# Attention products for heads of 64 value columns: two side-by-side parts in one stationary tile, two products instead of three

## The chip, the cores and the metric

The kernel runs on one core of one Trainium2 chip. Five engines of that core matter here: TensorE (PE; its weight loads are shown apart as PEld), VectorE (DVE), ScalarE (ACT), GpSimd (POOL) and SyncE (SP), which issues the weight transfers. The metric is the device time of one execution in microseconds (us).

## The reference

Two transformer blocks follow one another on one sequence of 512 tokens of width 1024, all in float32. What matters here is cut down to the attention of 64-wide heads:

- Block 1, branch a: 8 heads of 64 (block-sparse attention over two blocks of 256 tokens, causal, with a linear distance bias); with 512 tokens every earlier block is selected, so each head is plain causal attention. Branch b: 4 heads whose values are 128 wide (the difference of two softmaxes).
- Block 2: 4 heads of chunked gated linear attention whose values are 128 wide, and 8 heads of 64 (causal attention with a bias that counts three dilated windows).

```
p = softmax(q k^T / 8 + bias)          # per head, 512 x 512, causal
y[t, d] = sum_s p[t, s] v[s, d]        # d = 0..63 for the 16 heads of 64
```

Before and after the attention stand dense products (projections, gates, output products, two feed-forward layers of 2816).

## The kernel before

All tensors lie feature-major (features on the partitions, 512 tokens in the columns). To keep float32 accuracy on TensorE's faster fp32r path, every operand is split into an exact high and low part: ACT casts the high part (`nc.scalar.copy`), DVE subtracts it for the low part (`sub`, line 125). A product of two split operands is three TensorE products, hi·hi, hi·lo and lo·hi (`mm3`, line 142), each issued by `mm` (line 134, its instruction has line 137).

The weights of all dense products come as one stream of 512 KB chunks on SP's queue, and each half chunk is split by ACT (line 251) and DVE (line 125) up to three halves ahead of its use.

TensorE's order is fixed by the program (`pin` chains every PE instruction to the one before). It is worked out by a planner: tasks (generators) yield the time after which their next piece should be ready, `pump` issues the first task that is ready by the planner's clock `self.pt`, and fills with dense tile products when none is. `self.pt` grows by an estimated cost per PE instruction: for a product of n moving columns max(0.106, 0.216 n/512) us, for a transpose 0.108. ACT, DVE and POOL run their own queues in order, in an order that the framework sets from its own estimates; it need not be that of the program text.

For one 64-wide head the steps are these:

- `v_parts` (line 394) takes a projected value tile of two heads from PSUM. After four transposes into a `pt` bank, ACT casts `vh` (line 410, 128x512) and DVE subtracts for `vl`; both are token-major, 128 columns per block of 128 tokens, 64 for each head of the pair.
- `scores` and `normalise` make the probabilities `p` (one of three SBUF tiles of 1280 columns, handed on by `drop`).
- `att_v` (line 457) has four turns j = 0..3, one for each block of 128 keys. `turn(j)` transposes the probabilities of those keys into a `pt` bank (4 - j transposes), ACT casts them to `ph` (line 468) and DVE subtracts for `pl`. The turns 0 and 1 are issued ahead; then `av(j)` (line 452) adds three products into the single `y` bank, with 64 columns of `vh` or `vl` as the stationary tile and 512, 384, 256 and 128 moving columns for j = 0..3; after it `turn(j + 2)` is issued.
- At the end of a head ACT casts the high part of `y[:64]` (lines 556 in block 1, 1318 in block 2) and DVE subtracts for the low part, into the half `own` of the pair's tiles; then `p` is dropped and the next head may start its `att_v` (the resource `pv` is 1).

The heads with 128 value columns (`diff` in block 1, `gla` in block 2) use the same `av` with 128 stationary columns. In block 2 the last output product takes the eight k tiles in the order in which they are made, so the two products of the last pair of heads (`out`, line 1377) wait for the last head.

```
        qs = slice(128 * j, 512)
        c = slice(128 * j + cols.start, 128 * j + cols.stop)
        self.mm3(y[:, qs], (v[0][:, c], v[1][:, c]), (ph[:, qs], pl[:, qs]), j == 0, j == TB - 1)
...
            yield from self.att_v(p, box["v"], slice(64 * e, 64 * e + 64), y[:64])
            nc.scalar.copy(yh[own], y[:64])
            self.sub(yl[own], y[:64], yh[own])
```

Of the kernel before, what the change touches and what calls it, by code (L numbers as in the profile page):

```python
# [13 lines left out]
ALU = mybir.AluOpType  # L14
# [5 lines left out]
TB = S // 128  # L20
# [22 lines left out]
# cost of a transpose on the tensor engine, for the order in which its work is issued  # L43
# [3 lines left out]
class Done:  # L47
    """Marks a piece of work as issued; `at` is when its result should be there."""
# [10 lines left out]
class Item:  # L59
    """A dense tile product: runs whenever no task has tensor work that is ready."""  # L60
# [5 lines left out]
class Emitter:  # L66
# [25 lines left out]
    def phase(self, order=range(NSLOT)):  # L92
        """A part of the program with its own use of the working tiles."""
        self.slot, self.turn, self.free = {}, {}, list(order)
        self.pfree, self.pslot, self.res["prob"] = [0, 1, 2], {}, 3

    def W(self, tag, dt=F32, b=1, shape=(128, 512)):
        """A working tile; `b` of a tag take turns."""
        n = self.turn[tag] = self.turn.get(tag, -1) + 1
        key = (tag, n % b)  # L100
        if key not in self.slot:
            self.slot[key] = self.free.pop(0)
        return self.t(self.work, list(shape), dt, f"w{self.slot[key]}")

    def prob(self):
        """A tile for the probabilities of a head; free again after drop."""
        i = self.pfree.pop(0)
        p = self.t(self.work, [128, PW], F32, f"p{i}")
        self.pslot[id(p)] = i, p
        return p  # L110
# [31 lines left out]
    def mm3(self, out, l, r, first=True, last=True):  # L142
        """out (+)= l^T r from exact parts, (hi, lo) each."""
        self.mm(out, l[0], r[0], first, False)
        self.mm(out, l[0], r[1], False, False)
        self.mm(out, l[1], r[0], False, last)

# [61 lines left out]
    def pump(self, stop=None):  # L209
        """Issue until `stop()` (default: no tasks and no dense work are left)."""  # L210
# [29 lines left out]
    def _split(self, h):  # L240
        """Exact parts of half a chunk."""
# [30 lines left out]
    def mtile(self, ps, w, m, rhs, evac):  # L272
        """Generator: ps = W[:, m]^T rhs, then evac(ps); yields after each k."""
        n = len(rhs)
        for k in range(n):
            if k == 0 and ps is None:
                ps = self.bank()
            self.kstep(ps, w, m, k, rhs[k], k == 0, k == n - 1)
            yield 0.0
        return evac(ps)  # L280

    def kouter(self, cols, rhs, tags=("mm", "mm", "s", "s")):
        """Several tiles at once, k outermost: starts as soon as rhs[0] is there."""
        ps = [self.bank(tags[i]) for i in range(len(cols))]
        n = len(rhs)
# [10 lines left out]
    def colsum(self, ps, sq, first=True, last=True, c=0, tbs=range(TB)):  # L296
        """ps[:, 8 c + 2 tb] += per-token sums over the partitions of sq = (hi, lo), whose columns
        begin with the first of the token tiles tbs; the odd columns get the same."""
# [6 lines left out]
    def parts(self, full, dst=None):  # L305
        """(hi, lo) of a tile, for its sums."""
# [5 lines left out]
    def squares(self, x):  # L312
        """(hi, lo) of x^2, for its sums."""
        return self.parts(self.square(x))

    def gather(self, acc, sq):
        """acc += sq, beside the products; the first piece is the accumulator itself."""
# [5 lines left out]
    def after(self, ins, first):  # L323
        """Issue `ins` behind `first` on the engine that both run on."""
        self.tc.add_manual_dep(ins.ins, first.ins.name, NOSYNC, reason="order")

    def sums(self, ps, n=1, tbs=range(TB)):
        """The per-token sums that colsum left in the first n groups of columns."""
# [10 lines left out]
    def bcast(self, r):  # L339
        """[128 tokens, n] -> [128, 128 n], the same value on all partitions."""  # L340
# [34 lines left out]
    def qk_pair(self, q32, k32):  # L375
        """Stacked exact parts of two heads (rows 0-63 and 64-127) for the score products."""
# [17 lines left out]
    def v_parts(self, ps, rb=None, dst=None):  # L394
        """Task: token-major exact parts of a feature-major value tile in PSUM."""
# [8 lines left out]
        def go():  # L404
# [5 lines left out]
            nc.scalar.copy(vh, pt)  # L410
            self.sub(vl, pt, vh)
# [3 lines left out]
    def scores(self, h, qk, bias, out):  # L415
        """Task part: unnormalised probabilities [128, 1280] and 1/sum of one head."""
# [35 lines left out]
    def av(self, y, j, v, cols, ph, pl):  # L452
        qs = slice(128 * j, 512)
        c = slice(128 * j + cols.start, 128 * j + cols.stop)
        self.mm3(y[:, qs], (v[0][:, c], v[1][:, c]), (ph[:, qs], pl[:, qs]), j == 0, j == TB - 1)

    def att_v(self, p, v, cols, y):
        """Task part: y[d, q] = sum_s v[s, d] p[q, s] for one head."""
# [18 lines left out]
        for j in range(TB):  # L477
            self.av(y, j, v, cols, *parts[j])
# [5 lines left out]
    def block1_mix(self):  # L484
# [37 lines left out]
        def e_v(box):  # L522
            def f(ps):
                box["v"], g = self.v_parts(ps, rbx["b"])
# [15 lines left out]
        def moba(j, e, box):  # L540
# [12 lines left out]
            yield from self.att_v(p, box["v"], slice(64 * e, 64 * e + 64), y[:64])  # L553
            own = slice(64 * e, 64 * e + 64)
            yh, yl = ya[j]
            nc.scalar.copy(yh[own], y[:64])
            self.sub(yl[own], y[:64], yh[own])
# [4 lines left out]
        def diff(j, box):  # L562
# [23 lines left out]
            yield from self.att_v(p1, box["v"], slice(0, 128), y)  # L586
# [20 lines left out]
        # start: the first pair with k outermost, while x arrives; the norm follows  # L607
# [6 lines left out]
        for k, _ in enumerate(self.mtile(self.bank("s"), "w_in", 24, h, e_gate(0))):  # L614
# [4 lines left out]
            if k == 5:  # L619
# [4 lines left out]
                e_v(box[0])(ps[2])  # L624
# [6 lines left out]
        # lambda, the same on every partition  # L631
# [33 lines left out]
        for j in range(1, 8):  # L665
# [5 lines left out]
            self.dense(self.mtile(None, "w_in", o + 8 + jj, h, e_v(box[j])), gate)  # L671
# [33 lines left out]
    def bridge(self, w, rhs, g, slots, evac, chain, cols, h, tags=("mm", "s", "s", "y"), made=()):  # L705
        """The eight tiles of rhs @ W, the last g of them for the first and then for the other half of
        the tokens, and with h the first four tiles of the next stage, likewise: what the norm of one
        half waits for lies beside products of the other half. The weights of tiles that are used
        twice stay in `slots`. evac(m, c, ps) takes a tile (its columns c); chain(t, ps, done) is the
        task that takes the last tile of a half and makes that half of h; `made` are banks with the  # L710
        first tiles."""
# [65 lines left out]
    def block1_rest(self, mg):  # L777
# [98 lines left out]
        # modulation of block 2 on the vector engine, beside the products  # L876
# [49 lines left out]
        def chain(t, c, ps, done):  # L926
# [18 lines left out]
            # x + f g r has the squares' sum |x|^2 + 2 r x.fg + r^2 |fg|^2  # L945
# [39 lines left out]
    def ada(self, k, x, rb, i, dst, t=None):  # L985
        """Exact parts of x * rb * gm + shift, per feature."""
# [8 lines left out]
    def headsum(self, ps, sq):  # L995
        """ps[:, 2 tb + e] = per-token sums over the two halves of the partitions."""
# [4 lines left out]
    def block2_mix(self, x, h, ps):  # L1001
# [28 lines left out]
        # queries and keys of the linear attention, then its gates: 16 columns, all k in one tile  # L1030
# [74 lines left out]
        def gla(p):  # L1105
# [15 lines left out]
            def decayed(s):  # L1121
                """Keys of the first halves and queries of the second halves of all 2s tokens,
                decayed to and from the end of the first half."""
# [22 lines left out]
            def near(s, b):  # L1146
                """Parts for the pairs within 128 tokens; the queries of the two heads in columns
                of their own, with zeros in the other head's rows."""
# [19 lines left out]
            # the diagonal  # L1168
# [34 lines left out]
            for e in range(2):  # L1203
# [26 lines left out]
                for j in range(TB):  # L1230
                    self.av(y, j, gv[hd], slice(0, 128), *parts[j])
# [58 lines left out]
        def e_av(box):  # L1290
            def f(ps):
                box["v"], g = self.v_parts(ps)
# [3 lines left out]
        def dilated(j, e, box):  # L1296
# [16 lines left out]
            yield from self.att_v(p, box["v"], slice(64 * e, 64 * e + 64), y[:64])  # L1313
            if ya[j] is None:
                ya[j] = T(f"yah{j}", F32R), T(f"yal{j}", F32R)
            own = slice(64 * e, 64 * e + 64)
            yh, yl = ya[j]
            nc.scalar.copy(yh[own], y[:64])  # L1318
            self.sub(yl[own], y[:64], yh[own])
# [54 lines left out]
        # the first two tiles of the last product, their k in the order in which it comes  # L1374
# [147 lines left out]
def stream(inp, order):  # L1522
    """The 128x128 tiles of all dense weights in the order in which they are used."""
    w2 = inp["w_in_2"][0]
    w2 = np.concatenate([w2[:, :1536], w2[:, 1552:]], axis=1)
    # columns of block 2: gq gk gv gr aq ak av
# [11 lines left out]
def layout(g):  # L1538
# [16 lines left out]
    # constants of the shapes: key position minus query position, masked above the diagonal  # L1555
    d = (np.arange(512)[None, :] - np.arange(128)[:, None] - 384)
    o["dmast"] = np.where(d <= 0, d, -1e30).astype(np.float32)
    # eight times the log of how many of the three dilated windows hold the distance
# [3 lines left out]
    # pairs (key, query) of a 128-token block whose last common block of 2s tokens splits between them  # L1562
# [33 lines left out]
```

## Time and profile before

| | |
|---|---|
| time, median of 3 runs | 1505.06 us (1501.72 to 1508.11) |
| span of the profiled execution | 1504.9 us |
| mean granted TensorE clock | 0.985 |
| PE busy | 1451.4 us (96%), 7054 products and transposes |
| DVE busy | 934.4 us (62%) |
| ACT busy | 708.5 us (47%) |
| POOL busy | 307.7 us (20%) |
| DMA | 154.38 MB, mean 103 GB/s |

The span runs from the first to the last instruction of one profiled execution, on which all rows below are taken; it lies 0.2 us below the median of the runs. "Busy" counts the time in which at least one instruction of the engine was under way. PE's products are pipelined and overlap, so what one product costs the stream is read from start to start and not from its duration.

### The profile page before, as it was taken

Reading aid. Unit: us, or ns where it says so; the run is one execution under the profiler, and the core shown is the slowest. Engines: PE = TensorE matmul, PEld = TensorE weight load, DVE = VectorE, ACT = ScalarE, POOL = GpSimd, SP = SyncE. Lnnn points to the kernel's source line nnn. Section 1 sums busy time; section 2 is a strip of 40 time slices with the busy share of each in tenths; the row PEclk is TensorE's granted clock in tenths of the full one; section 3 lists DMA queues with packets and bytes.
Section 4 is the critical chain, followed back from the end, with each engine's and each line's share of the span. In section 5 each row is a group of like instructions: output and inputs, shape, how many; then the busy total and the mean of one; then the engine's idle time right before and its main releaser. Section 6 shows DMA issues by size and latency. Waiting matters only on the chain.

```text
span 1504.9 us, 19407 instructions
## 1 busy us (share of the span) xinstructions
PE 1451.4 (96%) x7054; PEld 1180.6 (78%) x7054; DVE 934.4 (62%) x1753; ACT 708.5 (47%) x1370; POOL 307.7 (20%) x285
## 2 busy tenths in 40 slices
PE   7999999999999999999998879899999999999998
PEld 6777777788988777888797667777779888888887
DVE  6655665656468888542548697766656766665322
ACT  5656655553643222332336546576546444444221
POOL 5322122101261111110314343412210111111000
PEclk9999999999999999999999987999999999999999
DMA  4221222224307887333234101121222233333331
GB/s 168 71 71 56 70 71 70 84 84 154 127 29 231 270 271 248 112 99 97 85 107 146 42 29 41 30 85 50 77 86 69 86 97 98 98 99 98 119 112 64
DMA packets 44592, 154.38 MB, mean 103 GB/s; under 512 B 5088, under 2 KB 5616, under 8 KB 44496
## 3 DMA queue, kind: packets, MB, share of 16 engines
q1 hardware_dynamic: 42944, 148.41, 31.6%
q0 software_dynamic: 1408, 4.59, 1.0%
q8 instruction: 55, 0.90, 0.2%
q14 instruction: 41, 0.34, 0.1%
q10 hardware_dynamic: 144, 0.14, 0.0%
HBM read 148.93 MB, written 4.19 MB: 102 GB/s over the span
## 4 chain that ended last, share of the span: by engine, by line
PE 74%; DVE 10%; issue 5%; DMA 4%; ACT 3%; POOL 3%; SPq 0%; DVEq 0%; POOLq 0%; ACTq 0%
PE mm L137 59%; PE s L137 8%; PE y L137 3%; DMA p<-w_ada 3%; DVE w L125 2%; PE pt L140 2%; POOL w L320 1%; DMA wraw<-w 1%; DVE wlo L125 1%; PE pc L137 1%; DVE w L891 1%; PE pt L137 1%; DVE w L1113 1%; ACT whi L251 1%; POOL rr L336 0%
## 5 line engine op out<-in xcount | busy, mean ns | idle before, releaser
L137 PE MATMUL mm<-hh,whi 128*128 128x512 f32 x1096 | 449.4, 410 | 12.6 <-ACT hh L370 7.0
L125 DVE TENSOR_TENSOR wlo<-wraw,whi 128x512 fp32r<-128x512 f32 x410 | 297.5, 729 | 252.4 <-ACT whi L251 248.7
L251 ACT CAST whi<-wraw 128x512 fp32r<-128x512 f32 x410 | 250.5, 620 | 399.4 <-PE mm L137 284.7
L137 PE MATMUL mm<-hl,whi 128*128 128x512 f32 x1096 | 431.3, 394 | 0.0
L137 PE MATMUL mm<-hh,wlo 128*128 128x512 f32 x1096 | 431.3, 394 | 0.0
L137 PE MATMUL mm<-w,whi 128*128 128x512 f32 (+1 forms) x984 | 281.5, 371 | 2.2 <-ACT w L1318 0.9
L137 PEld LDWEIGHTS mm<-hh,whi 128*128 128x128 f32 x1096 | 207.7, 189 | 69.5 <-issue 20.5
L137 PEld LDWEIGHTS mm<-hh,wlo 128*128 128x128 f32 x1096 | 207.7, 190 | 45.1
L137 PEld LDWEIGHTS mm<-hl,whi 128*128 128x128 f32 x1096 | 208.2, 190 | 36.2 <-DVE hl L371 0.6
L137 PEld LDWEIGHTS mm<-w,whi 128*128 128x128 f32 x984 | 177.4, 188 | 34.7 <-ACT w L1318 1.3
L137 PE MATMUL mm<-w,wlo 128*128 128x512 f32 (+1 forms) x492 | 181.5, 369 | 1.6 <-DVE wlo L125 1.6
L137 PEld LDWEIGHTS mm<-w,wlo 128*128 128x128 f32 x492 | 92.7, 188 | 17.5 <-DVE wlo L125 2.0
L137 PE MATMUL s<-w,w 128*128 128x128 f32 (+3 forms) x364 | 94.4, 352 | 8.1 <-DVE w L1196 5.2
L125 POOL TENSOR_TENSOR w<-w,w 64x512 fp32r<-64x512 f32 x48 | 66.6, 1387 | 142.4 <-ACT w L384 92.5
L137 PEld LDWEIGHTS s<-w,w 128*128 128x128 f32 x364 | 62.1, 206 | 39.8 <-issue 31.9
L891 DVE SCALAR_TENSOR_TENSOR w<-p,p 128x1024 bf16<-128x1024 f32 x48 | 63.7, 1327 | 20.5 <-DMA p<-w_ada 20.2
L125 DVE TENSOR_TENSOR w<-pt,w 128x512 fp32r<-128x512 f32 (+3 forms) x106 | 52.9, 505 | 34.5 <-ACT w L468 29.0
L1453 POOL TENSOR_TENSOR w<-w,w 128x512 f32<-128x512 f32 x22 | 29.0, 1319 | 205.6 <-ACT w L1452 205.5
L428 DVE CUSTOM_DVE_ANT_0 p<-s,w 128x128 f32<-128x128 f32 (+1 forms) x96 | 46.8, 488 | 35.4 <-PE s L137 34.7
L848 POOL TENSOR_TENSOR w<-w,w 128x512 f32<-128x512 f32 x22 | 28.6, 1304 | 193.6 <-ACT w L847 193.6
L320 POOL TENSOR_TENSOR w<-w,w 128x256 f32<-128x256 f32 (+1 forms) x43 | 48.8, 1138 | 91.6 <-ACT w L355 56.7
L125 DVE TENSOR_TENSOR w<-w,w 128x512 fp32r<-128x512 f32 (+3 forms) x107 | 59.5, 567 | 11.3 <-ACT w L859 4.8
(273 smaller groups left out, 1910.2 us busy)
## 6 DMA issues: line engine op xcount, KB each, us to landing
wraw<-w SPq DMA_DIRECT2D x220, 512.0 KB, 3.6
p<-w_ada SPq DMA_DIRECT2D x48, 512.0 KB, 4.4
x<-xT SPq DMA_DIRECT2D x8, 256.0 KB, 6.2
x<-xT POOLq DMA_DIRECT2D x8, 256.0 KB, 2.9
xd<-x SPq DMA_DIRECT2D x8, 256.0 KB, 2.5
x<-xd POOLq DMA_DIRECT2D x8, 256.0 KB, 2.9
outT<-x SPq DMA_DIRECT2D x7, 256.0 KB, 2.1
p<-c SPq DMA_DIRECT2D x1, 512.0 KB, 3.6
```

What stands on the lines that cost most here:

```text
L125: (eng or self.nc.vector).tensor_tensor(out=out, in0=full, in1=hi, op=ALU.subtract)
L137: self.pin(self.nc.tensor.matmul(out, lhsT=lhsT, rhs=rhs, start=start, stop=stop), us)
L140: self.pin(self.nc.tensor.transpose(out, in_, self.ident), USTR)
L251: self.nc.scalar.copy(hi, raw)
L320: self.nc.gpsimd.tensor_tensor(out=acc, in0=acc, in1=sq, op=ALU.add)
L428: nc.vector.tensor_tensor_reduce(out=p[:, OFF[i]:OFF[i] + w], in0=ps[:, :w], in1=bias[:, 384 - 128 * i:512], op0=ALU.add, op1=ALU.max, sca ...
L848: nc.gpsimd.tensor_tensor(out=g, in0=g, in1=sg, op=ALU.mult)
L891: nc.vector.scalar_tensor_tensor(out=junk, in0=wa, scalar=1.0, in1=cond, op0=ALU.mult, op1=ALU.mult, accum_out=self.mod[:, ni:ni + 1])
L1113: nc.vector.tensor_tensor_scan(c[:, o:o + n], self.one256[:, :n], la[p][:, o:o + n], 0.0, op0=ALU.mult, op1=ALU.add)
L1453: nc.gpsimd.tensor_tensor(out=u, in0=u, in1=sg, op=ALU.mult)
```

## The change

For the 16 heads of 64 value columns, the high and the low part of a head's values are laid side by side: 64 columns of high part and 64 of low part make one stationary tile of 128 columns for each block of 128 keys. `v_parts(heads=True)` now fills `vh` with head 0 (high and low) and `vl` with head 1, in four smaller operations instead of two. `av` then issues two products for each j, the tile with `ph` and with `pl`, instead of three; rows 0 to 63 of the `y` bank hold (vh·ph + vh·pl) and rows 64 to 127 hold (vl·ph + vl·pl). The new `y_parts` adds the two halves at the end: ACT copies the lower half to SBUF (into the head's own `p` tile), DVE adds the upper half, and high and low part are then cast and subtracted from that sum. The 128-wide heads keep three products. Besides, docstrings and comments are blanked.

```diff
-    def v_parts(self, ps, rb=None, dst=None):
+    def v_parts(self, ps, rb=None, dst=None, heads=False):
...
-            nc.scalar.copy(vh, pt)
-            self.sub(vl, pt, vh)
+            if heads:
+                pv = pt.rearrange("p (t e d) -> p t e d", e=2, d=64)
+                for e, t in enumerate((vh, vl)):
+                    tv = t.rearrange("p (t s d) -> p t s d", s=2, d=64)
+                    nc.scalar.copy(tv[:, :, 0], pv[:, :, e])
+                    self.sub(tv[:, :, 1], pv[:, :, e], tv[:, :, 0])
+            else:
+                nc.scalar.copy(vh, pt)
+                self.sub(vl, pt, vh)
...
-    def av(self, y, j, v, cols, ph, pl):
+    def av(self, y, j, v, ph, pl):
         qs = slice(128 * j, 512)
-        c = slice(128 * j + cols.start, 128 * j + cols.stop)
-        self.mm3(y[:, qs], (v[0][:, c], v[1][:, c]), (ph[:, qs], pl[:, qs]), j == 0, j == TB - 1)
+        c = slice(128 * j, 128 * j + 128)
+        if len(v) == 2:
+            self.mm3(y[:, qs], (v[0][:, c], v[1][:, c]), (ph[:, qs], pl[:, qs]), j == 0, j == TB - 1)
+        else:
+            self.mm(y[:, qs], v[0][:, c], ph[:, qs], j == 0, False)
+            self.mm(y[:, qs], v[0][:, c], pl[:, qs], False, j == TB - 1)
+
+    def y_parts(self, y, p, own, dst):
+        nc = self.nc
+        lo, y32 = p[own, :512], p[own, 512:1024]
+        nc.scalar.copy(lo, y[64:])
+        nc.vector.tensor_tensor(out=y32, in0=y[:64], in1=lo, op=ALU.add)
+        nc.scalar.copy(dst[0][own], y32)
+        self.sub(dst[1][own], y32, dst[0][own])
...
-            yield from self.att_v(p, box["v"], slice(64 * e, 64 * e + 64), y[:64])
-            own = slice(64 * e, 64 * e + 64)
-            yh, yl = ya[j]
-            nc.scalar.copy(yh[own], y[:64])
-            self.sub(yl[own], y[:64], yh[own])
+            yield from self.att_v(p, box["v"][e:e + 1], y)
+            self.y_parts(y, p, slice(64 * e, 64 * e + 64), ya[j])
             self.drop(p)
```

The last group stands once in `moba` (block 1) and once, in the same way, in `dilated` (block 2).

## Rows read from the trace of the kernel before

**Rows 1.** PE's busy time on the profile's page: us, share of the span, instructions.

```profile
PE 1451.4 (96%) x7054; PEld 1180.6 (78%) x7054; DVE 934.4 (62%) x1753; ACT 708.5 (47%) x1370; POOL 307.7 (20%) x285
```

**Rows 2.** Windows: length; busy us of PE, PEld, DVE, ACT, POOL; clock; DMA share; GB/s.

```profile
60.00:180.00 120.00, 119.41 (x576) 90.53 (x576) 71.04 (x159) 76.74 (x157) 26.22 (x18) 1.00 0.22 66
900.00:1090.00 190.00, 183.06 (x911) 142.71 (x910) 129.31 (x306) 115.50 (x261) 56.67 (x53) 0.92 0.19 56
1090.00:1103.00 13.00, 10.08 (x50) 6.28 (x51) 6.41 (x14) 7.35 (x20) 0.00 (x0) 1.00 0.00 0
```

**Rows 3.** Timeline of PE, one 64-wide head of block 1: start, us, operation, count.

```profile
99.36 0.86 PE L137 MATMUL y<-w,w 128*64 128x512 f32 x3
100.05 0.38 PE L140 MATMUL pt<-ident,p 128*128 128x128 f32 x2
...
101.64 0.69 PE L137 MATMUL y<-w,w 128*64 128x384 f32 x3
102.17 0.27 PE L140 MATMUL pt<-ident,p 128*128 128x128 f32 x1
...
103.66 0.51 PE L137 MATMUL y<-w,w 128*64 128x256 f32 x3
104.01 0.40 PE L137 MATMUL mm<-hh,whi 128*128 128x512 f32 x1
...
105.40 0.34 PE L137 MATMUL y<-w,w 128*64 128x128 f32 x3
105.57 0.44 PE L137 MATMUL mm<-hh,whi 128*128 128x512 f32 x1
```

**Rows 4.** Timeline of PE, two groups of a 128-wide head of block 1.

```profile
204.03 0.85 PE L137 MATMUL y<-w,w 128*128 128x512 f32 x3
204.72 0.38 PE L140 MATMUL pt<-ident,p 128*128 128x128 f32 x2
...
210.09 0.45 PE L137 MATMUL y<-w,w 128*128 128x128 f32 x3
210.37 0.44 PE L137 MATMUL mm<-hh,whi 128*128 128x512 f32 x1
```

**Rows 5.** Groups by line and shape: count; total us, mean ns; idle before it.

```profile
L125 DVE TENSOR_TENSOR w<-y,w 64x512 fp32r<-64x512 f32 x16 | 10.9, 682 | 7.4 <-ACT w L556 3.9 <-ACT w L1318 3.3
...
L410 ACT CAST w<-pt 128x512 fp32r<-128x512 f32 x14 | 8.2, 585 | 24.1 <-PE pt L140 24.1
...
L468 ACT CAST w<-pt 128x256 fp32r<-128x256 f32 x20 | 7.4, 369 | 21.6 <-PE pt L140 21.0 <-DVE w L125 0.6
```

**Rows 6.** Timeline, all engines, end of one head and start of the next.

```profile
133.44 0.57 ACT L556 CAST w<-y 64x512 fp32r<-64x512 f32 x1
...
135.27 0.59 ACT L468 CAST w<-pt 128x512 fp32r<-128x512 f32 x1
...
136.41 0.68 DVE L125 TENSOR_TENSOR w<-y,w 64x512 fp32r<-64x512 f32 x1
...
137.02 1.14 DVE L125 TENSOR_TENSOR w<-pt,w 128x512 fp32r<-128x512 f32 x2
...
138.78 0.86 PE L137 MATMUL y<-w,w 128*64 128x512 f32 x3
```

**Rows 7.** The chain that ended last, end of block 2's attention: start, us, what.

```profile
1089.91 2.30 ACT p L438 x8
...
1093.71 0.68 PE y L137 x2
...
1100.95 0.59 ACT w L1318
...
1101.56 0.70 DVE w L125
```

**Rows 8.** The same chain within the gated linear attention.

```profile
965.43 2.26 DVE w L125 x2
```

**Rows 9.** Timeline of DVE at that place.

```profile
967.01 0.67 DVE L125 TENSOR_TENSOR w<-y,w 64x512 fp32r<-64x512 f32 x1
```

More of the change, by code (lines that the diff above doesn't have):

```diff
@@ L450, in normalise, with att_v @@
                 self.nc.vector.tensor_scalar(blk, blk, rs[:, i:i + 1], None, op0=ALU.mult)
-    def av(self, y, j, v, cols, ph, pl):
+    def av(self, y, j, v, ph, pl):
         qs = slice(128 * j, 512)
-        c = slice(128 * j + cols.start, 128 * j + cols.stop)
-        self.mm3(y[:, qs], (v[0][:, c], v[1][:, c]), (ph[:, qs], pl[:, qs]), j == 0, j == TB - 1)
-    def att_v(self, p, v, cols, y):
+        c = slice(128 * j, 128 * j + 128)
[11 more added lines that the diff above has]
+        self.sub(dst[1][own], y32, dst[0][own])
+    def att_v(self, p, v, y):
         nc = self.nc
@@ L477, in att_v @@
         for j in range(TB):
-            self.av(y, j, v, cols, *parts[j])
+            self.av(y, j, v, *parts[j])
             if j + 2 < TB:
@@ L520, in e_q, with e_v @@
             return f
-        def e_v(box):
+        def e_v(box, heads):
             def f(ps):
-                box["v"], g = self.v_parts(ps, rbx["b"])
+                box["v"], g = self.v_parts(ps, rbx["b"], heads=heads)
                 self.add(g, box["vd"])
@@ L585, in diff @@
             y = self.bank("y")
-            yield from self.att_v(p1, box["v"], slice(0, 128), y)
+            yield from self.att_v(p1, box["v"], y)
             yr = T("ybr")
@@ L623, in block1_mix @@
                 box[0]["kd"].at = self.pt + 1.0 + e_q(box[0], "k")(ps[1])
-                e_v(box[0])(ps[2])
+                e_v(box[0], True)(ps[2])
         o = VEC_COLS["g_ffn_post"][0]
@@ L670, in block1_mix @@
             box[j]["kd"] = self.dense(self.mtile(None, "w_in", o + 4 + jj, h, e_q(box[j], "k")), gate)
-            self.dense(self.mtile(None, "w_in", o + 8 + jj, h, e_v(box[j])), gate)
+            self.dense(self.mtile(None, "w_in", o + 8 + jj, h, e_v(box[j], j < 4)), gate)
             self.add(pair(j))
@@ L1230, in gla @@
                 for j in range(TB):
-                    self.av(y, j, gv[hd], slice(0, 128), *parts[j])
+                    self.av(y, j, gv[hd], *parts[j])
                     if j + 2 < TB:
@@ L1291, in f @@
             def f(ps):
-                box["v"], g = self.v_parts(ps)
+                box["v"], g = self.v_parts(ps, heads=True)
                 self.add(g, box["vd"])
@@ L1312, in dilated @@
             y = self.bank("y")
-            yield from self.att_v(p, box["v"], slice(64 * e, 64 * e + 64), y[:64])
+            yield from self.att_v(p, box["v"][e:e + 1], y)
             if ya[j] is None:
                 ya[j] = T(f"yah{j}", F32R), T(f"yal{j}", F32R)
[L1316 to L1319, printed above, removed]
+            self.y_parts(y, p, slice(64 * e, 64 * e + 64), ya[j])
             self.drop(p)
```

## The prediction

> **What bounds the kernel now.** I read the page first. PE is busy for 1451.4 of 1504.9 us, DVE and ACT for 934.4 and 708.5 [rows 1]. A share of 96% does not yet say that a saved product is saved time, so I went stage by stage with the windows. The reader should see three different places in which the 16 heads of 64 run. The eight heads of block 1 lie in a stretch of 120 us in which PE is busy for 119.41 us, DVE and ACT for 71 and 77: PE alone sets the pace there. Six heads of block 2 start between 900 and 1090 us, where PE is busy for 183.06 of 190 us at a mean clock of 0.92, so PE sets the pace for most of the time, but not for all of it. The last two heads lie between 1090 and 1103 us, where PE is busy for 10.08 of 13 us and everything else for less: that is a chain of waits, and no engine is full [rows 2]. So the change has to be priced three times.
>
> The third view is PE's timeline, because durations of overlapping products can't be added. From the start of a group of three products to the start of the next instruction, the four groups of a 64-wide head take 0.69, 0.53, 0.35 and 0.17 us for 512, 384, 256 and 128 moving columns, 1.74 us in all [rows 3]. The fourth view is the chain that ended last, for the two places where PE is not the bound [rows 7, 8].
>
> **The change part by part.**
>
> *Products.* Each head loses four of twelve products. The trace has the new form already, in the 128-wide heads: three products with 128 stationary columns take 0.69 us at 512 moving columns, as much as with 64, but 0.28 us at 128 against 0.17 [rows 3, 4]. So the stationary width is free at 512 and costs at 128. For 384 and 256 I take the price per product of the 64-wide head, since three such products there go by columns (0.53 and 0.35 of 0.69 are close to 3/4 and 1/2). Two products then cost 0.46, 0.35 and 0.23 us for the first three groups. For the last group the bounds are two thirds of 0.17, which is 0.11 (the wider load is hidden behind the dense product ahead), and 0.28 (nothing gained); I take two thirds of the 128-wide price, 0.19, the row of the same shape. Together 1.23 us, a saving of 0.51 us for a head, between 0.41 and 0.58. Over 16 heads that is 8.1 us, 6.6 to 9.3 at the bounds.
>
> The row of the 128-wide group, 0.28 us for three products of only 128 columns, says that something other than the moving columns paces them [rows 4]. The Trainium skill, "TensorE: Matmul & The Clock Gate", section "LDWEIGHTS (loading the stationary operand)", says that a weight load takes as long as it has columns, P/1.2 ns, which speaks against this change: fewer products, but two loads of 128 columns where there were three of 64. By that rule two products of the last group cost 0.21 us as an estimate from the page, more than the 0.17 of today, the saving is 0.48 us for a head, and the sum of 16 heads is 7.7 instead of 8.1 us.
>
> *Where that saving counts.* Block 1, eight heads in a full PE stretch: -4.1 us. Block 2: of the six heads that start before 1090 us I count five in full, -2.6 us. The first of them ends while DVE leads the chain: the step at 965.43 is two DVE operations of 2.26 us, one of which, from 967.01, is that head's subtraction from `y` [rows 8, 9]. There PE's saving is worth nothing, and the new addition lengthens the step: the nearest row, the subtraction of the same 64x512 shape from PSUM, takes 0.68 us [rows 5]. I take +0.7, between -0.5 (the order of DVE's queue hides it) and +2 (addition, cast and subtraction all land on the chain). In the last two heads PE's products stand on the chain between DVE's and ACT's steps; the 0.68 us step at 1093.71 is the two products that wait for `pl` [rows 7], of which one goes. I count 0.5 and 0.4 us for the two, -0.9; the bounds are 0 and -1.2.
>
> *The end of a head.* Before: one ACT cast (0.57 us) and one DVE subtraction (0.68 us) [rows 5, 6]. After: ACT copy, DVE addition, ACT cast, DVE subtraction, one behind the other. The high part comes later by an addition and a cast, 0.68 + 0.58 us, and two hand-overs of about 0.03 us (0.02 between 1101.54 and 1101.56 [rows 7]): 1.3 us. The `y` bank is free as early as before, since the addition, its last reader, stands where the subtraction stood. What hides the 1.3 us: nothing reads the high part until the output product, except in the last pair; and the next head's first turn has room. In one of the tightest hand-overs ACT casts `y` at 133.44, casts the next head's first turn at 135.27, and PE first reads that at 138.78, 2.9 us after it is ready. DVE's half of that turn is ready at about 137.7, 1.3 us before the second product wants it at 139.0 [rows 6]. Without that cover each head would cost 1.3 us.
>
> The cover is gone in one place for certain: the output product's last k waits for the last head. There the chain runs ACT 0.59, DVE 0.70 [rows 7], and 1.3 us come on top: +1.3. Earlier on the chain, at 1089.91, ACT runs eight pieces of softmax, 2.30 us, right behind the end of a head [rows 7]; the new second cast may be put among them: +0.3, between 0 and +0.6.
>
> *Values.* ACT's cast of 128x512 at 0.585 us becomes two of 256 columns at 0.369 each: +0.15 us of ACT for each of 8 tiles, and about the same for DVE [rows 5]. In block 1 ACT and DVE are idle for over a third of the stretch [rows 2], so that costs nothing; without the cover it would be 0.3 us a tile. The `p` tile is held some 2 us longer; there are three, and a new head waits 2 us by plan before it writes.
>
> *The planner* takes off 0.59 us a head, close to the 0.51 that go, so its order should stay sensible; some pieces will change places, which I can't price beyond a us or two either way.
>
> *Sum.* -4.1 - 2.6 + 0.7 - 0.9 + 1.3 + 0.3 = -5.3 us. On the profiled 1504.9 us that is 1499.6; the median lies 0.2 us above the span, so 1499.8 us, -0.35%. The time moves by less than 0.5%, about what a measurement of this kernel can tell from no change (its three runs spread over 6.4 us): 0.5% is 7.5 us, so "faster" begins below 1497.5 and "slower" above 1512.6.
>
> **The rivals.**
>
> *All of it arrives.* The late high part and the longer DVE work are hidden everywhere, and the loads of the last group too: 8.1 us, at the bound 9.3: 1497 us, down to 1495.8. For it: PE's 96% [rows 1] and 2.9 us of room at a hand-over [rows 6]. Against it: the last head's chain, which nothing covers [rows 7]. Chance 0.25.
>
> *Eaten in block 2.* Block 1 gives its 4.1 us, and the stretch from 900 to 1103 us, where DVE leads at times and PE's clock falls to a mean of 0.92 when it waits [rows 2], gives all of it back: +2 us at the first head, the tail at its upper bounds (1.3 + 0.6, no saving in the two heads), and half of the five heads' 2.6 us lost: -4.1 - 1.3 + 2 + 1.9 = -1.5 us, and a change of order may take the rest: about 1503 to 1507 us. For it: the step at 965.43 [rows 8]. Against it: only two or three places. Chance 0.13.
>
> *ACT stands behind DVE: slower.* The new second cast waits on ACT for an addition on DVE. In the row at 136.41 DVE reached the subtraction of `y` 2.4 us after ACT's cast had ended at 134.01 [rows 6]; if the addition waits like that, ACT stands, and the next head's cast of its first turn stands behind it, for which PE waits. It decides from the point where the delay passes the 1.3 us of room before the product that reads `pl`; if 1.3 us then come on PE's path in each of 16 heads, that is 20.8 - 8.1 = +12.7 us, 1517.8 us. The Trainium skill, "Perfetto Trace Analysis", section "Tensor Engine Instruction (MATMUL, LD_WEIGHTS)", says that ACT and DVE are strict first-in, first-out, which is what would make this happen. Against it: the row of 136.41 is the longest such wait that I found in block 1, and the queue's order is free to put other casts ahead. Chance 0.06.
>
> **How the numbers follow.** The forecast, a partial gain between 1497.5 and 1503.5 us, has 0.56; with the eaten case the "same" chance is 0.69, "faster" 0.25, "slower" 0.06. The predicted time is the sum's, 1499.8 us. The range runs from 1495.8, the bound of the full gain, to 1507, the top of the eaten case; it leaves out the slower rival and a little beside the ends.
>
> **What would show it.** Products into `y`: 64 fewer in all, 7054 to 6990 on PE. The groups of a 64-wide head in block 1: two products, 0.46, 0.35, 0.23 and 0.19 us from start to start. Additions of 64x512 on DVE near 0.68 us, 16 of them; second casts near 0.6 us. The end of block 2's attention: from the last product into `y` to the output product that reads the high part, ACT, DVE, ACT, 1.3 us longer than today. PE's waits between 60 and 180 us stay under 1 us in all. I am wrong if PE waits for ACT's casts of the turns in block 1 (the slower rival), if the two-product group of 128 columns costs 0.28 us, or if the stretch from 900 to 1090 us changes by more than 3 us either way.

## The result

The changed kernel takes 1518.17 us (median of 9 runs, 1512.52 to 1521.53) against 1505.06 us for the kernel before (9 runs, 1500.35 to 1512.94). The ratio is 1.0074, with a 95% interval of 1.0051 to 1.0097. It is slower by about 0.7%; 1499.8 us was forecast, with a range from 1495.8 to 1507.

The page of the changed kernel, its span and the busy times of the engines (compare [rows 1]):

```profile
span 1519.6 us, 19323 instructions
...
PE 1454.2 (96%) x6990; PEld 1187.1 (78%) x6990; DVE 952.2 (63%) x1777; ACT 720.5 (47%) x1394; POOL 304.6 (20%) x285
```

The 64 products are gone, 6990 instead of 7054, and yet PE is busy for 2.8 us longer. Busy time is therefore not work: fewer products took longer, at a mean granted clock of 0.976 over the profiled execution against 0.985 before. The windows of the same kernel (columns as in [rows 2]):

```profile
60.00:180.00 120.00, 119.27 (x557) 92.14 (x556) 82.65 (x176) 83.14 (x170) 25.30 (x18) 1.00 0.22 66
200.00:220.00 20.00, 18.42 (x90) 14.88 (x90) 10.99 (x19) 8.36 (x16) 6.40 (x5) 1.00 0.23 68
...
240.00:260.00 20.00, 18.42 (x83) 15.10 (x82) 10.38 (x18) 7.68 (x14) 6.40 (x5) 0.91 0.21 66
...
280.00:300.00 20.00, 18.42 (x83) 15.24 (x82) 10.19 (x16) 8.66 (x16) 6.38 (x5) 0.91 0.34 104
...
900.00:1090.00 190.00, 183.83 (x884) 145.26 (x885) 134.99 (x316) 118.77 (x261) 58.31 (x57) 0.89 0.19 56
1090.00:1103.00 13.00, 7.24 (x24) 4.55 (x24) 6.10 (x21) 8.44 (x24) 0.00 (x0) 0.79 0.00 1
```

The kernel before in the three windows between 200 and 300 us:

```profile
200.00:220.00 20.00, 20.00 (x101) 16.64 (x100) 11.40 (x19) 9.29 (x17) 7.00 (x5) 1.00 0.29 84
...
240.00:260.00 20.00, 19.43 (x97) 15.94 (x96) 11.34 (x21) 8.99 (x17) 6.43 (x5) 1.00 0.29 87
...
280.00:300.00 20.00, 20.00 (x98) 15.76 (x97) 11.96 (x26) 8.99 (x17) 6.41 (x5) 1.00 0.35 105
```

The first row of the changed kernel is the stretch of the 64-wide heads in block 1, and PE is as full there as before. The loss is elsewhere. Three windows between 200 and 300 us, in block 1's 128-wide heads, which the change does not touch, have 1.58 us without PE each, two of them a clock of 0.91; before, PE stood for 0.57 us in one of them, at 1.00 in all. At the end of block 2's attention PE works for 7.24 of 13 us where it was 10.08, at 0.79 instead of 1.00 [rows 2]. (That window is the same time, not the same work: the changed kernel comes to this place some 5 us later.)

**Where the time went, by stage.** The 5064 products with a weight tile of the dense layers are the same, in the same order, in all the kernels below. So the start of the n-th of them, less its start in the profiled execution before, says how late a kernel is at that point, and the difference of two such points says what the stage between them lost or gained. In us, worked out from the traces (e1 to e11 are the experiments; e8 is the kernel before, profiled again):

```
products       200   200-  600- 1000- 1600- 2400- 3130- 3385- 3415-
                to     600  1000  1600  2400  3130  3385  3415   end
starts at     70.2   to    to    to    to    to    to    to    to
(before)             204.9 330.3 493.4 683.3 981.9 1078.2 1105.2 1500.1
after         +0.4   -3.8  +8.3  +0.1  +3.3  -1.5  -1.5  +8.6  +0.9
e1            +1.9   -2.6   0.0  +1.2  +2.6  -5.1  -0.7  +9.7  +0.8
e2            +0.8    0.0  +9.7  +0.3  +2.4 -10.0  -0.2  +1.0  -0.1
e3            +1.0   -3.9  +9.7   0.0  +2.8  -6.3   0.0  +0.2  +0.1
e4            +2.8    0.0   0.0  +0.3  +2.1  -4.6  -1.6  +8.6  +0.6
e5            +2.6   -3.9  -0.5  +1.7  +1.7  -1.5  -1.5  +8.6  +0.8
e6            +0.4   -2.7   0.0  +0.5  -1.5  -2.5  -0.7  +5.1  +0.5
e7            +1.5   -2.8   0.0  -0.2  +0.8  -0.1  -0.3   0.0  -0.3
e8            +0.1    0.0   0.0   0.0  +3.2  -6.5   0.0   0.0  -0.1
e9            +0.5   -3.9  -0.5  +1.5  +2.2  -1.5  -1.0   0.0  +0.1
e10           +2.2   -3.9  -0.5  +1.7  -0.5  -5.8  +0.1   0.0  +0.1
e11           +1.0    0.0  -1.3  +1.1  +3.5   0.0  +0.1   0.0  -0.1
```

Read the row of e8 first. Two executions of one program agree to 0.1 us in block 1's attention (200 to 1000), in most of block 2's (3130 to 3415) and in the last feed-forward layers. They differ by 3.2 us in block 1's feed-forward and by 6.5 us in the gated linear attention. In those two columns, and in the start, nothing can be read of a change. One repetition is little, but the other kernels bear it out where they leave a stage as it was: e2, e4 and e11 are within 0.1 us in column 200 to 600, e3, e7, e9, e10 and e11 within 0.2 us in column 3385 to 3415.

The products into `y` between these points show which heads a column holds (but for a group at an edge). Column 200 to 600 has seven of block 1's eight 64-wide heads (the first lies ahead of it), column 600 to 1000 the four 128-wide heads. Column 3130 to 3385 has the third, fourth and fifth of block 2's 64-wide heads and two 128-wide ones, column 3385 to 3415 the sixth to eighth; the first two lie in the gated linear attention. So the changed kernel gains 3.8 us in seven heads of block 1, loses 8.3 us in the 128-wide heads after them, gains 1.5 us in three heads in the middle of block 2 and loses 8.6 us in the last three.

**The loss in block 1.** PE's waits in the changed kernel from 200 to 330 us (us in total, times, longest):

```profile
PE pc L137 <- DVE sql L125: 4.7, 3, 1.6
```

These are the products that sum the squares of a 128-wide head. PE, DVE and POOL at the first of the three places (timeline: start, us):

```profile
210.81 1.86 DVE L388 CAST w<-w 64x512 fp32r<-64x512 f32 x2
...
210.93 2.87 POOL L125 TENSOR_TENSOR w<-w,w 64x512 fp32r<-64x512 f32 x2 [5.08 <-ACT w L387]
...
212.66 0.17 PE L137 MATMUL pc<-ones,sqh 128*128 128x2 f32 x1
212.70 1.65 DVE L125 TENSOR_TENSOR sql<-sq,sqh 128x512 fp32r<-128x512 f32 x1
...
214.40 0.27 PE L137 MATMUL pc<-ones,sql 128*128 128x2 f32 x1 [1.58 <-DVE sql L125]
```

The reader should see two delays one upon the other. DVE does the casts of the next pair's keys (1.86 us) before it comes to `sql`, the low part of the squares. Then `sql` takes 1.65 us: POOL is at work until 213.80, and `sql` ends 0.55 us after it. In the kernel before, DVE did `sql` ahead of the casts and ahead of POOL, and PE had `sql` in time:

```profile
213.29 0.68 DVE L125 TENSOR_TENSOR sql<-sq,sqh 128x512 fp32r<-128x512 f32 x1
...
213.52 1.59 POOL L125 TENSOR_TENSOR w<-w,w 64x512 fp32r<-64x512 f32 x1 [5.08 <-ACT w L387]
...
214.00 1.39 DVE L388 CAST w<-w 64x512 fp32r<-64x512 f32 x1
```

Nothing of the change runs at this place. What changed is the order written by the planner, which now counts a 64-wide head as shorter.

**The loss at the end of block 2's attention.** Timeline of the changed kernel:

```profile
1095.25 0.40 ACT L446 ACTIVATE p<-p,nm 128x128 f32<-128x128 f32 x1 [1.19 <-DVE nm L442]
...
1097.56 0.58 ACT L474 COPY p<-y 64x512 f32<-64x512 f32 x1
...
1098.16 1.12 ACT L456 ACTIVATE p<-p,rs 128x256 f32<-128x256 f32 x2
1098.43 0.69 DVE L475 TENSOR_TENSOR p<-y,p 64x512 f32<-64x512 f32 x1
1099.31 0.61 ACT L476 CAST w<-p 64x512 fp32r<-64x512 f32 x1
...
1099.98 1.52 PE L137 MATMUL mm<-w,whi 128*128 128x512 f32 x2 [4.42 <-ACT w L476]
...
1103.00 1.27 PE L140 MATMUL pt<-ident,p 128*128 128x128 f32 x5
```

The head that ends here is the sixth of eight. Its copy stands on ACT behind the eight pieces of the next head's softmax (from 1095.25), its second cast behind the next head's normalisation (1098.16). PE has the output products that read this head's high part next in its written order, ahead of the last two heads' transposes. So PE stands for 4.42 us. The transposes read the next head's probabilities, whose normalisation on ACT ended at 1099.28; they start only at 1103.00, behind the six products. The chain that ended last has both:

```profile
1095.25 2.29 ACT p L446 x8
1099.98 3.22 PE mm L137 x6
1114.62 2.50 PE mm L137 x5
```

The last of the six products start 0.43 us apart, where the dense products of block 1 start 0.23 us apart; between 1099 and 1103 us the granted clock was 0.50, the lower of its two levels (1.2 of 2.4 GHz). After the last head PE waits again, 2.04 us up to 1113.90, and the clock from 1113 to 1118 us was 0.66.

### The profile page after: what moved, and what is told of

It reads as the page before. It is cut to its first block, busy times and chain, and to the rows that moved or that the text cites. A ratio compares the mean times of both kernels' runs of the same rounds, so it can differ in the third digit from the quotient of the medians.

```text
span 1519.6 us, 19323 instructions
## 1 busy us (share of the span) xinstructions
PE 1454.2 (96%) x6990; PEld 1187.1 (78%) x6990; DVE 952.2 (63%) x1777; ACT 720.5 (47%) x1394; POOL 304.6 (20%) x285
## 4 chain that ended last, share of the span: by engine, by line
PE 75%; DVE 9%; issue 4%; ACT 4%; DMA 4%; POOL 3%; SPq 0%; DVEq 0%; POOLq 0%; ACTq 0%
PE mm L137 61%; PE s L137 8%; PE y L137 2%; PE pt L140 2%; DMA p<-w_ada 2%; DVE w L125 2%; POOL w L320 2%; PE pc L137 1%; DMA wraw<-w 1%; DVE wlo L125 1%; PE pt L137 1%; DVE w L911 1%; DVE sql L125 1%; ACT whi L251 1%; POOL rr L336 1%
## 5 line engine op out<-in xcount | busy, mean ns | idle before, releaser
L125 DVE TENSOR_TENSOR w<-pt,w 128x256 fp32r<-128x256 f32 (+3 forms) x114 | 53.9, 480 | 32.9 <-ACT w L491 27.6
```

The source lines that it names most:

```text
L125: (eng or self.nc.vector).tensor_tensor(out=out, in0=full, in1=hi, op=ALU.subtract)
```

## The experiments

The ratios are to the kernel before, timed on the same chip beside each batch (medians 1504.43, 1504.95 and 1506.39 us).

**e1, all of the change, PE in the order of before.** The planner is told that the removed product still costs what it did:

```diff
             self.mm(y[:, qs], v[0][:, c], pl[:, qs], False, j == TB - 1)
+            self.pt += max(0.106, 0.216 * (512 - 128 * j) / 512)
```

> The changed kernel, but the planner still charges the product that is gone, so TensorE's order is exactly that of the kernel before, less 64 products. Order theory (the planner's shifted clock puts the squares' sum of the 128-wide heads of block 1 where VectorE is late; three waits of 1.6 us and a lower clock after them): the dense product number 1000, where block 1's attention ends, comes 3.4 to 4.1 us earlier than in the kernel before instead of 4.9 us later; the whole lands 7 to 9 us under the changed kernel, about 1510 us. Rival, extra work theory (the additions, casts and longer chains on ScalarE and VectorE cost the time wherever they stand, the order is incidental): no more than 2 us better than the changed kernel, about 1517 us.

1513.46 us (1509.15 to 1516.69), ratio 1.0050 [1.0032, 1.0068]. Apart from the products into `y`, PE's order is that of before instruction by instruction. Products 600 to 1000 take the time of before, as the order theory had it. The rest of its numbers missed: the heads of block 1 gain 2.6 us, not 3.4 to 4.1, the tail is later by 1.1 us than in the changed kernel (9.7 against 8.6), and the time falls by 4.7 us, not by 7 to 9. The windows of e1, the same stretches as above:

```profile
200.00:220.00 20.00, 20.00 (x101) 16.54 (x99) 11.50 (x19) 9.04 (x17) 7.01 (x5) 1.00 0.27 80
...
240.00:260.00 20.00, 19.43 (x99) 15.87 (x97) 11.41 (x21) 8.73 (x16) 6.43 (x5) 1.00 0.29 89
...
280.00:300.00 20.00, 20.00 (x98) 15.68 (x96) 12.16 (x26) 9.02 (x16) 6.40 (x5) 1.00 0.38 106
```

**e2, the kernel before, PE in the order of after.** All three products are made, and the third is not charged for 64 columns:

```diff
+        at = self.pt
         self.mm(y[:, qs], v[1][:, c], ph[:, qs], False, j == TB - 1)
+        if cols.stop - cols.start == 64:
+            self.pt = at
```

> The kernel before with its three products and its old end of a head, but the planner does not charge the third product of a 64-wide head, so TensorE's order is exactly that of the changed kernel. Order theory: the loss in block 1 appears without any of the new work, product number 1000 comes 6 to 9 us late (no saving, all of the waits), the whole about 1512 us. Extra work theory: within 2 us of the kernel before, about 1505 us.

1514.72 us (1510.44 to 1519.21), ratio 1.0067 [1.0042, 1.0092]: nearly as slow as the change, with not one instruction of it, and PE in the changed kernel's order throughout. (The profiled execution was the shortest of the six; its row has -10.0 us in the gated linear attention.) Block 1 loses 9.7 us between 600 and 1000, somewhat more than the 6 to 9 expected, PE's waits for `sql` from 200 to 330 us are 4.8 us in 3, and the tail is late by 1.0 us only.

**e3 and e4, the change in one block alone.** In the other block the heads have three products and the old end.

> The change in block 1 alone; block 2 keeps three products and its old end of a head. Order theory and tail theory (the late high part costs 8 us at the end of block 2's attention) together: product number 1000 is 4.9 us late as in the changed kernel, and nothing is added at the end of block 2's attention: about 1510 us. Extra work theory: half of the 13 us, spread, about 1511 us, so this run alone does not tell the two apart; with the next one it shows whether the parts add up.

> The change in block 2 alone; block 1 is the kernel before. Tail theory: up to the last pair of heads 2 to 3 us are saved, then 8 us are lost within 25 us around the last output product's wait for the high part: about 1510 us, and block 1 as before (product number 1000 within 0.5 us). Rival, the loss in block 2 is spread over its eight heads by the extra VectorE and ScalarE work: no step of more than 3 us in any 30 us.

e3: 1511.43 us, ratio 1.0046 [1.0028, 1.0065]. e4: 1510.09 us, ratio 1.0041 [1.0019, 1.0064]. e3 has the gain of 3.9 us and the loss of 9.7 us in block 1, and an undisturbed tail; e4 has an untouched block 1 and the tail's 8.6 us. The two losses are independent, one in each block, and each is larger than what its block saves.

**e5, late sums.** One due time of the planner's, in the 128-wide heads:

```diff
             sq = self.squares(yr)
-            yield 2.5
+            yield 5.0
             pc = self.bank("pc")
             self.colsum(pc, sq)
```

> The changed kernel with one figure of the planner's altered: in the heads of 128 value columns the products that sum the squares are due 5.0 us after the squares, not 2.5, so PE's written order has them later. No work is added or removed. Order theory: the loss in block 1 comes from these products standing in PE's order ahead of the squares that they need; it goes, the stretch from product 600 to 1000 of the dense layers takes the time it takes before (within 2 us, not 8.3 us more), and the time falls from 1518 to 1508 to 1512, with the tail of block 2 still some 9 us late. Rival (the idle time there is due to DVE or ACT being late whatever PE's order is): the stretch stays 6 to 10 us longer and the time stays at 1516 to 1520.

1506.81 us (1504.32 to 1515.15), ratio 1.0024 [1.0003, 1.0045], lower than expected; the execution that was profiled took 1514.68 us. Products 600 to 1000 take 0.5 us less than before, not 8.3 more, and PE no longer waits for `sql` there, although `sql` is as slow as it was in two of its four places (line, then least, median and most ns):

```profile
L125 DVE TENSOR_TENSOR sql<-sq,sqh x4: 692/1242/1667, 214.8 to 327.0; 128x512 fp32r<-128x512 f32 x4
```

So the delay of `sql` costs nothing if PE has other products in front of the one that reads it. The tail stays at +8.6 us.

**e6, late k6.** e1, with the six output products of the third pair moved behind the last pair's heads in PE's written order:

```diff
                     yield att[2 * k - 7]
+                    if k == 6:
+                        yield att[6]
+                        yield att[7]
```

> The first experiment's kernel (all of the change, PE in the order of before) with one move in PE's written order: in block 2 the six output products that take the second-last pair of heads stand behind the last pair's heads. Tail theory, PE's order: PE idled because these products stood next while their operand, the pair's low part, was cast late; the lateness of the tail (dense products 3390 to 3420) falls from 9.7 us to 2 to 4 us, and the time from 1513.5 to 1506 to 1509. Tail theory, ACT's queue alone: whatever PE has next, ACT's eight softmax pieces ahead of the copy hold up the last pair too; the tail stays at 7 us or more and the time at 1511 to 1515.

1505.42 us (1501.82 to 1510.73), ratio 1.0006 [0.9989, 1.0023]. The tail falls from 9.7 to 5.1 us, between the two theories' numbers, and the time to below the first's. The rest is seen in the timeline of e6:

```profile
1085.01 0.70 ACT L446 ACTIVATE p<-p,nm 128x512 f32<-128x512 f32 x1
...
1085.83 0.58 ACT L475 COPY p<-y 64x512 f32<-64x512 f32 x1
...
1086.44 1.12 ACT L456 ACTIVATE p<-p,rs 128x256 f32<-128x256 f32 x2
...
1087.58 0.58 ACT L492 CAST w<-pt 128x512 fp32r<-128x512 f32 x1
...
1088.22 1.51 PE L137 MATMUL y<-w,w 128*128 128x512 f32 x2 [3.41 <-ACT w L492]
```

ACT's queue, with the head's new copy in it, now holds up the next head's first turn. PE stands for 3.41 us, where in e1 it stood for 3.8 and, behind the last head, for 2.0 us; and from 1088 to 1101 us it is busy for 12.74 of 13 us, at a clock of 0.50. PE's written order was thus about half of the tail, 4.6 of 9.7 us. That ACT's order, with the clock after it, is the rest is read from this timeline and was not tested by itself, and how the 5.1 us divide between the wait and the clock was not separated. Neither theory alone holds: each took one of the two orders for the whole cause.

**e7, the last two pairs of block 2 in the form of before.** Built on e1:

```diff
-            yield from self.att_v(p, box["v"][e:e + 1], y)
-            self.y_parts(y, p, slice(64 * e, 64 * e + 64), ya[j])
+            if j < 2:
+                ...
+            else:
+                own = slice(64 * e, 64 * e + 64)
+                yield from self.att_v(p, (*box["v"], own), y[:64])
+                yh, yl = ya[j]
+                nc.scalar.copy(yh[own], y[:64])
+                self.sub(yl[own], y[:64], yh[own])
```

> The first experiment's kernel (all of the change, PE in the order of before) with pairs 2 and 3 of block 2, the four last heads, in the form of before: three products, no add, copy and subtraction at the end. Order and tail theory together: 12 heads keep their saving of about 0.5 us, both losses are gone: tail under 1.5 us late, time 1499 to 1503, 2 to 5 us under before. Rival (the new end of a head costs as much as the products save, wherever the head stands): no gain, 1504 to 1507.

1501.29 us (1499.36 to 1506.43), ratio 0.9978 [0.9960, 0.9996], inside what was expected. The tail is not late at all. Block 1 gains 2.8 us. Of the four first heads of block 2 the third and fourth lie where a change can be read; they gain 0.3 us, where two heads at the forecast's 0.51 would gain 1.0.

**e8, the kernel before again.** One profile.

> The kernel before, unaltered, for one profile: how far the stages' times differ between two executions of the same program. Expected: attention stretches within 1 us of the first profile, the start and the feed-forward layers within 1 to 3 us, the scan of the gated layers within some 5 us, since these moved in every run so far, with no part of the change in them.

1503.28 us. The expectation held for the attention stretches and nearly for block 1's feed-forward (3.2 us); the gated linear attention moved by 6.5 us, a little more than expected.

**e9 to e11, the two losses taken out.** e9 is the changed kernel with e5's due time and e7's old form of the last two pairs; e10 is e3 with e5's due time; e11 is the kernel before with e5's due time.

> All of the change but in the four last heads of block 2 (form of before), the planner charging what is issued, and its sums of squares due 5.0 us after the squares as in the fifth experiment. If the two losses are all there is: block 1 ends some 4 us early (product 1000 against product 200), the tail is not late, time 1499 to 1502. If the four first heads of block 2 gain nothing (they gained 0.3 us in the seventh experiment, of 2.0 forecast), the tenth experiment, without them, comes out within 1 us.

> The change in block 1 alone (all of block 2 in the form of before), the sums of squares due 5.0 us after the squares. Order theory: block 1 is some 4 us shorter, where the third experiment, the same but for that figure, was 5.8 us longer; time 1499 to 1502. Rival (the idle time in block 1 comes from the heads' new form): as the third experiment, 1510 to 1513.

> The kernel before with nothing of the change, only its sums of squares due 5.0 us after the squares: what that figure does alone. If it only mends a wrong order that the change brought on, 1504 to 1506, no change; if the order of before has slack there too, 1501 to 1503, and then what the ninth and tenth gain is partly not the change's.

e9: 1499.25 us (1495.22 to 1504.58), ratio 0.9953 [0.9933, 0.9974], the fastest of all and inside what was expected. Its page:

```profile
PE 1449.7 (97%) x7006; PEld 1182.8 (79%) x7006; DVE 949.0 (63%) x1771; ACT 719.9 (48%) x1390; POOL 305.7 (20%) x285
```

In the three windows of block 1 that were shown for the other kernels PE is busy for 20.00 of 20 us each, at a clock of 1.00.

e11: 1507.21 us, ratio 1.0013 [0.9991, 1.0034], so the due time by itself gains nothing that can be measured in the whole. In its own stage, products 600 to 1000, the row of e11 shows 1.3 us less than before; up to that much of what e9 and e10 gain in block 1 may be the due time's and not the change's. e10: 1502.26 us, just above what was expected, ratio 0.9984 [0.9963, 1.0005], not told apart from no change, though its block 1 is 4.4 us shorter (3.9 in the 64-wide heads, 0.5 in the 128-wide). Whether the four first heads of block 2, which e9 has and e10 has not, are worth the 3 us between the two medians stays open: the intervals overlap. The two of them that can be read, in column 3130 to 3385, gain 1.0 us in e9, which is what two heads were forecast to gain.

## Why the prediction was wrong, point by point

**Right: the products.** In block 1 the groups of one changed head, the same as in [rows 3], are these (timeline of PE, the changed kernel):

```profile
98.94 0.62 PE L137 MATMUL y<-w,w 128*128 128x512 f32 x2
99.40 0.38 PE L140 MATMUL pt<-ident,p 128*128 128x128 f32 x2
...
101.01 0.52 PE L137 MATMUL y<-w,w 128*128 128x384 f32 x2
101.36 0.27 PE L140 MATMUL pt<-ident,p 128*128 128x128 f32 x1
...
102.86 0.39 PE L137 MATMUL y<-w,w 128*128 128x256 f32 x2
103.09 0.40 PE L137 MATMUL mm<-hh,whi 128*128 128x512 f32 x1
...
104.46 0.33 PE L137 MATMUL y<-w,w 128*128 128x128 f32 x2
104.63 0.45 PE L137 MATMUL mm<-hh,whi 128*128 128x512 f32 x1
```

From start to start 0.46, 0.35 and 0.23 us, as forecast; the group of 128 columns takes 0.17 in each of block 1's eight heads, not 0.19, and not the 0.21 of the page's rule. That makes 1.21 us for a head and a saving of 0.53. The seven heads of block 1 in column 200 to 600 gain 3.8 to 3.9 us in the planner's new order, where seven at 0.51 are 3.6.

The 16 additions take 683 ns each, the second casts 617:

```profile
L475 DVE TENSOR_TENSOR p<-y,p 64x512 f32<-64x512 f32 x16 | 10.9, 683 | 6.4 <-ACT p L474 6.3
...
L476 ACT CAST w<-p 64x512 fp32r<-64x512 f32 x16 | 9.9, 617 | 5.6 <-DVE p L475 5.3
```

**Right: the hand-overs of block 1.** PE's waits between 60 and 180 us are these two, 0.7 us in all, under the 1 us that was named:

```profile
PE y L137 <- ACT w L491: 0.5, 1, 0.5
PE y L137 <- DVE w L125: 0.2, 1, 0.2
```

So the slower rival, ACT behind DVE in each of 16 heads, did not happen, though the time came out within 0.4 us of its 1517.8. That nearness is chance. Nor is the loss at the end of block 2 its mechanism: there the second cast stood behind ACT's own work, which ran from 1095.25 to 1099.28 us almost without a break, while the addition on DVE had ended at 1099.12.

**Right: block 2's middle, as far as it can be read.** Of the five heads that were to gain 2.6 us, three lie in column 3130 to 3385: 1.5 us at the forecast's price, and the changed kernel, e4 and e5 gain 1.5, 1.6 and 1.5. The half of this saving that the eaten case took off was not lost. With the planner's old charge the heads give less, in both blocks: 2.6 and 2.8 us of 3.6 in block 1 (e1, e7), 0.7 of 1.5 in block 2 (e1, e6). So an order planned for the old cost keeps part of the saving from arriving; why was not tested. The +0.7 us at the first head lies in the gated linear attention, which varies by 6.5 us of itself, and stays open.

**Wrong, one of two steps of like size: the planner.** The text has it that the charge is "close to the 0.51 that go, so its order should stay sensible; some pieces will change places, which I can't price beyond a us or two either way". The pieces that changed places cost 8.3 us. e2 shows it without the change's work, e1 and e5 show it gone with all of that work in place. The mistake was to look for the price of an edit in the heads that it touches only. The order of all that comes after shifts too, and from 200 us on there stood products whose operand was ready just in time. The trace of before had the sign: between 200 and 330 us PE waited once for `sql`, 0.6 us, and at the place shown above DVE's casts stood right behind it, with POOL starting 0.23 us after `sql`.

```profile
PE pc L137 <- DVE sql L125: 0.6, 1, 0.6
```

**Wrong, the other step: what hides the late high part.** That "nothing reads the high part until the output product, except in the last pair" holds by the data and fails by PE's order. The output products of the third pair too stand ahead of the last pair's transposes in that order, so whoever makes them late makes everything behind them late. The term was +1.3 +0.3 - 0.9 = +0.7 us for the whole tail; measured were 8.6 in a column that also holds the sixth head, which was to save 0.5. The last head's own price was well sized. From the start of ACT's step on `y` to PE's product it is 0.63 us before (1100.95 to 1101.58) and 2.00 us after (ACT 1111.90, DVE 1112.51, ACT 1113.23, PE 1113.90), 1.37 us more. The +0.3 for a cast "among" the softmax pieces was the step that failed: copy and cast were put behind eight pieces and a normalisation, 2.29 and 1.12 us, and the upper bound of 0.6 did not think of that.

**The clock.** Nothing was set down for it, though [rows 2] showed 0.92 for a stretch with waits. In the changed kernel two of the three stops of 1.58 us in block 1 lie in windows with a clock of 0.91, and behind the stop of 4.42 us the clock was 0.50. For block 1 the parts can be added up, as an estimate that counts the share by which the mean clock lies under 1.00 as lost time, since PE is full outside the waits. PE waited 4.7 us for `sql` where it had waited 0.6, which is 4.1 us; two windows of 20 us at 0.91 lack 1.8 us each; together 7.7 of the 8.3 us. In e2, which lost 9.7 us, PE waited 4.2 us more, and three windows were at 0.91:

```profile
220.00:240.00 20.00, 20.00 (x79) 14.38 (x78) 10.86 (x33) 11.08 (x26) 2.44 (x2) 0.91 0.09 27
...
260.00:280.00 20.00, 20.00 (x81) 14.40 (x81) 10.15 (x33) 10.15 (x25) 1.04 (x1) 0.91 0.08 27
...
300.00:320.00 20.00, 19.53 (x79) 14.08 (x80) 10.47 (x31) 9.20 (x22) 1.01 (x1) 0.91 0.09 27
```

That is 4.2 + 5.4 = 9.6 of the 9.7 us. So the wait for `sql` and the lower clock behind it are nearly the whole loss of block 1, and e2 loses more than the changed kernel because one more of these 20 us has the lower clock (1.8 us, of a difference of 1.4). At the end of block 2 the two were not separated.

## What to carry to other kernels

Where a program writes the order of an engine's work from planned costs, an edit that makes a piece cheaper reorders everything behind it: run the new order with the old work, and the old order with the new work, before the edit is judged. A result that comes later by 1.3 us is free only if nothing that stands in the consumer engine's queue ahead of independent work reads it; look for the first reader in that queue, not for the first reader in the data. And look for products that stand just behind their operand: those decide what a reordering costs.

## What the runs showed of the hardware

A DVE subtraction with both inputs in SBUF took 0.68 us when it began before POOL's subtraction and 1.65 us when POOL was already at work, and it ended 0.55 us after POOL did (214.35 and 213.80). The same holds in all 13 traces: in the 32 cases in which POOL was at work when `sql` began, `sql` took between 0.93 and 1.67 us and ended 0.55 or 0.56 us after POOL each time; in the other 20 it took 0.68 or 0.69 us. So it looks as if it had waited for POOL, and was not slowed. The Trainium skill, "SBUF — State Buffer", section "SBUF: two separate sides", says that the two engines share one pair of ports, which the one that starts first holds for its whole instruction while the other is blocked (for a DVE operation with two SBUF inputs, where POOL's reads SBUF); these rows agree, and no experiment here took POOL's work away to show it.

A stretch of 13 us at a clock of 0.50, with PE busy for 12.74 of it (e6, 1088 to 1101 us), shows that PE can be nearly full and still be granted half its pace for that long. Before it PE had stood for 1.34 and 3.41 us within 7 us.
